# Three of eight row pairs of two matrix products by Strassen's algorithm, with all sums on VectorE

## The chip, the cores and the metric

One NeuronCore of a Trainium2 chip runs the whole program. The metric is the device time of one execution in microseconds (us). TensorE (PE) multiplies matrices into eight PSUM banks; VectorE (DVE) and ScalarE (ACT) do everything elementwise; GpSimd (POOL) does little here; SyncE (SP) issues the loads of the weights.

## The reference

The program is a trunk of two layers on x of 256 rows by 2048 columns (float32). Each layer has two halves:

```
u = RMSNorm(x)
proj = u @ w_in                                   # 2048 -> 8256
y_a = MLA(c_q, c_kv, k_pe) @ w_o_mla              # 8 heads
y_b = neighbourhood_attention(q, k, v) @ w_o_na   # 8 heads
merged = sigmoid(gate_a) * y_a + sigmoid(gate_b) * y_b
x = x + merged @ w_out                            # 2048 -> 2048
h = RMSNorm(x) @ w_ff1                            # 2048 -> 8192
x = x + square(relu(h)) @ w_ff2                   # 8192 -> 2048
```

A final RMSNorm gives the output.

## The kernel before

Matrix products are done in float32 from two rounded parts: a value is a high part (`hi`, a cast by ScalarE to the format that TensorE multiplies) and a low part (`lo`, value minus high part, by VectorE). A product takes high x high, high x low and low x high.

Weights come in blocks of 1 MB, by SyncE, into one of three `raw` tiles. `weights` (L157 and on) casts two rows of 128 k at a time: ScalarE writes `hi` (L172), VectorE `lo` (L173), each 128 x 1024, four tiles of either kind. Activations stand as `pair` tiles, high part and low part side by side, in 44 slots.

Two routines multiply. `gemm_a` (L215) holds the activations fixed in the array and streams 512 columns of weights: for each of 16 rows of k and each half t of the 256 rows three matmuls (L199, L200, L201) into one of two banks, 96 in all. It is used for the gates, the output projections, `w_out` and `w_ff2`, that is, for all products whose result has its rows on the partitions. `gemm_b` (L227) streams the activations against weights held fixed (L194, L195) into four banks; it makes the hidden values of the MLP, and the queries and keys.

The MLP goes in four blocks of 2048 hidden columns: four calls of `gemm_b` with w_ff1, whose results `relu2` squares and splits, and then four calls of `gemm_a` with w_ff2, whose results `residual` adds to x with the squared norm scale (L619, one instruction for each bank). For w_out the sum is L617.

Small steps that other work must not wait for (transposes of the merged branches and of x, attention heads, norm scales) are generators in a list; `tick`, called between matmuls, advances one of them when its lag has passed, and `drain` runs them all. In this way the transposes of each quarter of `merged` start while the next quarter is still being multiplied, and the scales of a layer's norm are made while the next layer's first product runs. Three banks (`abank`) are kept for these steps and five for the products.

The order of instructions on each engine is set afterwards by a scheduler, which takes dependences, free buffers and its own estimates; each engine runs its list in that order.

Of the kernel before, what the change touches and what calls it, by code (L numbers as in the profile page):

```python
# [54 lines left out]
NSLOT, ABANKS, SMALL, RBUFS, HBUFS = 44, 3, 8, 3, 4  # L56
# [6 lines left out]
def trunk(ctx: ExitStack, tc: tile.TileContext, x, w_in, w_uq, w_ukv, rpb, w_o_mla, w_o_na,  # L63
# [3 lines left out]
    wpool = ctx.enter_context(tc.tile_pool(name="wpool", bufs=4))  # L67
    slots = ctx.enter_context(tc.tile_pool(name="slots", bufs=NSLOT))
    tmp = ctx.enter_context(tc.tile_pool(name="tmp", bufs=2))
    psum = ctx.enter_context(tc.tile_pool(name="psum", bufs=8, space=bass.MemoryType.PSUM))  # L70

    def bank():
        return psum.tile([P, 512], F32, tag="bank", name="bank", bufs=8 - ABANKS)

    def abank():
        return psum.tile([P, 512], F32, tag="abank", name="abank", bufs=ABANKS)
# [8 lines left out]
    def small():  # L85
        return tmp.tile([P, S], F32, tag="small", name="small", bufs=SMALL)
# [70 lines left out]
    def weights(w, nk, c0, n, before=None):  # L157
# [3 lines left out]
        for k0 in range(0, nk, 2):  # L161
# [6 lines left out]
            hi = wpool.tile([P, 1024], F32R, tag="hi", name="hi", bufs=HBUFS)  # L168
            lo = wpool.tile([P, 1024], F32R, tag="lo", name="lo", bufs=HBUFS)
# [6 lines left out]
    def weights_twice(w, nk, c0, n):  # L176
# [4 lines left out]
        for k0 in range(0, nk, 8):  # L181
            hi = wpool.tile([P, 1024], F32R, tag="hi", name="hi", bufs=HBUFS)
            lo = wpool.tile([P, 1024], F32R, tag="lo", name="lo", bufs=HBUFS)
# [58 lines left out]
    def rows_of(col):  # L242

        dg = [tmp.tile([P, P], F32, tag="diag", name="diag", bufs=4) for _ in range(2)]
# [6 lines left out]
        row = tmp.tile([P, S], F32, tag="rrow", name="rrow", bufs=4)  # L251
        nc.vector.tensor_copy(row, pb[:, :S])
        return row

    def root(v, width, name):

        nc.vector.tensor_scalar(v, v, 1.0 / width, EPS, op0=ALU.mult, op1=ALU.add)  # L257
        col = tmp.tile([P, 2], F32, tag="rcol", name=name, bufs=6)
# [3 lines left out]
    class Norm:  # L262
# [5 lines left out]
        def add(self, t):  # L268
# [6 lines left out]
            nc.gpsimd.tensor_tensor(self.acc, self.acc, sq, op=ALU.add)  # L275

        def scales(self):
# [5 lines left out]
            v = tmp.tile([P, 2], F32, tag="var", name="var", bufs=2)  # L283
# [4 lines left out]
    class RowNorm:  # L288


        def __init__(self):
            self.sums = tmp.tile([P, 2, 4], F32, tag="sums", name="sums", bufs=2)

        def add(self, t, c4):
            junk = tmp.tile([P, 512], F32, tag="junk", name="junk", bufs=1)
# [3 lines left out]
        def scale(self):  # L299
            v = tmp.tile([P, 2], F32, tag="var", name="var", bufs=2)  # L300
# [3 lines left out]
        def scales(self):  # L304

            self.scale()
            self.half = tmp.tile([P, 2], F32, tag="rcol", name="half", bufs=6)
# [3 lines left out]
        def square(self):  # L311

            self.scale()
            self.sq = tmp.tile([P, 2], F32, tag="rcol", name="sq", bufs=6)
            nc.vector.tensor_tensor(self.sq, self.col, self.col, op=ALU.mult)
            return
            yield
# [157 lines left out]
    for l in range(DEPTH):  # L475
        wi = w_in[l]
# [116 lines left out]
        mg = [None] * NC  # L593
        for c4 in range(4):
            th = [None] * 2

            def merge(t, ps):
# [3 lines left out]
                if t == 1:  # L601
                    start(turned(lambda t, c4=c4: part[t, c4], c4, mg, lambda c: 0.5), 2)
# [4 lines left out]
            gemm_a(w_o_mla[l], c4 * 512, att, merge)  # L607


        last = l == DEPTH - 1  # L610

        def residual(c4, scale=None, n=None, then=None):

            def evac(t, ps):
                cs = xt[t][:, c4 * 512:(c4 + 1) * 512]
                if scale is None:
                    nc.vector.tensor_tensor(cs, cs, ps, op=ALU.add)  # L617
                else:
                    nc.vector.scalar_tensor_tensor(cs, ps, scale.sq[:, t:t + 1], cs, op0=ALU.mult, op1=ALU.add)  # L619
                if n is not None:  # L620
                    n.add(t, c4)
                if then is not None and t == 1:
                    start(then(c4), 2)
# [4 lines left out]
        for c4 in range(4):  # L628
            gemm_a(w_out[l], c4 * 512, mg,
                   residual(c4, None, mlp, lambda c4, xg=xg: turned_x(c4, xg, G_MLP + l * NC)))  # L630
        start(mlp.square(), 10)
# [4 lines left out]
        for b in range(NB):  # L636
            hid = []

            def relu2(m, ps):
                t = whole(ps)  # L640
                nc.vector.scalar_tensor_tensor(t, t, 0.0, t, op0=ALU.max, op1=ALU.mult)  # L641
                a = pair()
                split(a, t)
                hid.append(a)

            for c4 in range(4):
                gemm_b(w_ff1[l], b * D + c4 * 512, xg, relu2)
            for c4 in range(4):
                if b < NB - 1:
                    ev = residual(c4, mlp)  # L650
                elif last:
                    ev = residual(c4, mlp, norm)
                else:
                    ev = residual(c4, mlp, norm, lambda c4, nxt=nxt: turned_x(c4, nxt, G_MIX + (l + 1) * NC))
                gemm_a(w_ff2[l][b * D:(b + 1) * D, :], c4 * 512, hid, ev)
            if last and b == NB - 2:
                gfin = [wide() for _ in range(4)]
                for c4 in range(4):
                    nc.gpsimd.dma_start(gfin[c4], gain_fin[:, c4 * 512:(c4 + 1) * 512].to_broadcast([P, 512]))
        xg = nxt  # L660
        if not last:
            start(norm.scales(), 10)

# [67 lines left out]
```

## Time and profile before

| | |
|---|---|
| time, median of 3 runs (lowest to highest) | 2689.91 us (2688.54 to 2690.1) |
| the profiled execution's own time | 2689.91 us |
| its span in the profile | 2688.1 us |
| busy, PE / DVE / ACT / POOL | 2666.8 / 1602.9 / 1277.1 / 60.5 us |
| HBM traffic | 492 MB read, 184 GB/s over the span |

The own time holds 1.8 us around the span. "Busy" counts the union of an engine's instructions. Matmul rows overlap one another, so the cost of one is the step from start to start. In a group's row, the count is followed by busy time and mean length of one, then by the engine's idle time just before these instructions and by what ended it.

### The profile page before, as it was taken

The page shows a single profiled execution, that of the slowest core. Times are in us where ns is not written, and L with a number is a line of the kernel's source. Part 1 is how long each engine was busy: PE and PEld are TensorE (multiplying, and loading weights), DVE is VectorE, ACT ScalarE, POOL GpSimd, SP SyncE. Part 2 cuts the span into 40 slices and gives each one's busy share as a digit, 9 for nine tenths or more (in the row PEclk, how much of TensorE's full clock was granted, in tenths as well). Part 3 has the DMA queues.
Part 4 walks back from the last instruction along what each step waited for, and adds up shares of the span by engine and source line. Part 5 has one row for each costly group of instructions (what it writes and reads, how often), then busy time and mean ns, then how long its engine had stood idle before and what let it go on. Part 6 is the DMA issues. An engine that isn't in the chain of part 4 may idle for free.

```text
span 2688.1 us, 34037 instructions
## 1 busy us (share of the span) xinstructions
PE 2666.8 (99%) x13596; PEld 2268.7 (84%) x13596; DVE 1602.9 (60%) x2158; ACT 1277.1 (48%) x1815; POOL 60.5 (2%) x86
## 2 busy tenths in 40 slices
PE   8999999999999999999999999999999999999998
PEld 7888888888888888888888888888888888888886
DVE  5676486555655546556567754955556555565554
ACT  5554465444434434444445544644444344443443
POOL 1110000000000000000001100000000000000000
PEclk9999999999999999999999999999999999999999
DMA  7555644555565555555555555455555555655554
GB/s 231 184 165 189 195 161 155 189 184 180 186 203 186 190 190 186 197 193 189 183 183 179 171 187 183 153 167 188 188 188 188 189 187 194 208 189 193 188 188 141
DMA packets 253839, 496.49 MB, mean 185 GB/s; under 512 B 12688, under 2 KB 16784, under 8 KB 253680
## 3 DMA queue, kind: packets, MB, share of 16 engines
q1 hardware_dynamic: 250624, 488.14, 55.2%
q0 software_dynamic: 2048, 4.56, 0.6%
q8 instruction: 106, 1.74, 0.3%
q10 hardware_dynamic: 1008, 1.61, 0.2%
q14 instruction: 53, 0.43, 0.0%
HBM read 492.18 MB, written 2.10 MB: 184 GB/s over the span
## 4 chain that ended last, share of the span: by engine, by line
PE 84%; issue 14%; DVE 1%; DMA 1%; ACT 0%; POOL 0%; SPq 0%; POOLq 0%; DVEq 0%; ACTq 0%
PE bank L194 21%; PE bank L199 16%; PE bank L200 16%; PE bank L201 16%; PE bank L195 11%; DMA raw<-in_w_in 1%; PE abank L206 1%; PE abank L205 1%; PE abank L204 1%; PE abank L326 1%; PE abank L377 0%; DVE lo L173 0%; DVE wide L670 0%; PE abank L347 0%; ACT hi L172 0%
## 5 line engine op out<-in xcount | busy, mean ns | idle before, releaser
L173 DVE TENSOR_TENSOR lo<-raw,hi 128x1024 fp32r<-128x1024 f32 (+1 forms) x928 | 1132.5, 1222 | 977.8 <-ACT hi L172 973.0
L172 ACT CAST hi<-raw 128x1024 fp32r<-128x1024 f32 (+1 forms) x928 | 971.8, 1049 | 1131.1 <-PE bank L201 736.2
L194 PE MATMUL bank<-pair,hi 128*128 128x512 f32 x3008 | 1059.0, 398 | 2.3 <-DVE small L212 1.0
L200 PE MATMUL bank<-lo,pair 128*128 128x512 f32 (+1 forms) x2240 | 866.1, 387 | 0.0
L199 PE MATMUL bank<-hi,pair 128*128 128x512 f32 (+1 forms) x2240 | 865.8, 388 | 0.0
L201 PE MATMUL bank<-hi,pair 128*128 128x512 f32 (+1 forms) x2240 | 865.8, 387 | 0.0
L195 PE MATMUL bank<-pair,lo 128*128 128x256 f32 x3008 | 835.5, 280 | 0.4 <-DVE lo L173 0.3
L194 PEld LDWEIGHTS bank<-pair,hi 128*128 128x128 f32 x3008 | 563.5, 188 | 133.0 <-ACT hi L172 1.9
L195 PEld LDWEIGHTS bank<-pair,lo 128*128 128x128 f32 x3008 | 567.7, 189 | 5.9 <-DVE lo L173 1.6
L201 PEld LDWEIGHTS bank<-hi,pair 128*128 128x128 f32 x2240 | 420.8, 188 | 84.6
L199 PEld LDWEIGHTS bank<-hi,pair 128*128 128x128 f32 x2240 | 420.8, 188 | 84.1
L200 PEld LDWEIGHTS bank<-lo,pair 128*128 128x128 f32 x2240 | 420.9, 188 | 82.6
L150 ACT ACTIVATE pair<-small 128x256 fp32r<-128x256 f32 x200 | 73.6, 413 | 89.8 <-DVE small L641 67.1
L210 ACT COPY small<-bank 128x256 f32<-128x256 f32 x218 | 78.6, 369 | 29.0 <-PE bank L195 27.8
L152 DVE TENSOR_TENSOR pair<-small,pair 128x256 fp32r<-128x256 f32 x200 | 76.6, 418 | 19.2 <-ACT pair L150 19.2
L212 DVE TENSOR_TENSOR small<-bank,small 128x256 f32<-128x256 f32 x218 | 83.0, 416 | 0.2
L259 POOL TENSOR_TENSOR col<-var,mhalf 128x2 f32<-128x2 f32 x9 | 6.3, 702 | 1928.8 <-DVE var L257 1928.8
L619 DVE SCALAR_TENSOR_TENSOR xt<-bank,sq,xt 128x512 f32<-128x512 f32 x64 | 45.0, 744 | 7.8 <-PE bank L201 7.8
L641 DVE SCALAR_TENSOR_TENSOR small<-small 128x256 f32<-128x256 f32 x128 | 48.2, 418 | 0.0
L154 DVE SCALAR_TENSOR_TENSOR pair<-abank,g_sb,pair 128x256 fp32r<-128x256 f32 x64 | 29.2, 478 | 23.0 <-ACT pair L150 23.0
L150 ACT ACTIVATE pair<-abank,g_sb 128x256 fp32r<-128x256 f32 x64 | 28.2, 469 | 27.3 <-PE abank L326 23.4
L150 ACT ACTIVATE pair<-abank 128x256 fp32r<-128x256 f32 x64 | 23.6, 381 | 29.2 <-PE abank L206 19.1
(96 smaller groups left out, 789.9 us busy)
## 6 DMA issues: line engine op xcount, KB each, us to landing
raw<-in_w_ff SPq DMA_DIRECT2D x256, 1024.0 KB, 5.0
raw<-in_w_in SPq DMA_DIRECT2D x124, 1024.0 KB, 5.1
raw<-in_w_out SPq DMA_DIRECT2D x32, 1024.0 KB, 4.9
raw<-in_w_o_na SPq DMA_DIRECT2D x16, 1024.0 KB, 4.9
raw<-in_w_o_mla SPq DMA_DIRECT2D x16, 1024.0 KB, 4.9
raw<-in_w_ukv SPq DMA_DIRECT2D x8, 1024.0 KB, 4.9
raw<-in_w_uq SPq DMA_DIRECT2D x8, 768.0 KB, 4.6
raw<-in_w_in SPq DMA_DIRECT2D x10, 512.0 KB, 4.9
```

The lines of the kernel that those rows point to most:

```text
L150: nc.scalar.activation(dst[:, :S], src, AF.Copy, scale=scale)
L152: nc.vector.tensor_tensor(dst[:, S:], src, dst[:, :S].bitcast(F32), op=ALU.subtract)
L172: nc.scalar.copy(hi, src)
L173: nc.vector.tensor_tensor(lo, src, hi.bitcast(F32), op=ALU.subtract)
L194: nc.tensor.matmul(ps, wh, a, start=first, stop=False)
L195: nc.tensor.matmul(ps[:, :S], wl, a[:, :S], start=False, stop=last)
L199: nc.tensor.matmul(ps, a[:, t * P:(t + 1) * P], wh, start=first, stop=False)
L200: nc.tensor.matmul(ps, a[:, t * P:(t + 1) * P], wl, start=False, stop=False)
L201: nc.tensor.matmul(ps, a[:, S + t * P:S + (t + 1) * P], wh, start=False, stop=last)
L210: nc.scalar.copy(h, ps[:, S:])
L212: nc.vector.tensor_tensor(t, ps[:, :S], h, op=ALU.add)
L641: nc.vector.scalar_tensor_tensor(t, t, 0.0, t, op0=ALU.max, op1=ALU.mult)
```

## The change

**The products.** `gemm_s` takes the place of `gemm_a` for w_out and w_ff2, on 1024 columns at a time, so each of these products is two calls (g = 0, 1) where it was four. It goes through eight pairs of k rows. Pairs 0, 1, 3, 5 and 7 are plain: 24 matmuls into four banks (numbers 2, 3, 4, 8). Pairs 2, 4 and 6 (`SPAIRS`) take the 2 x 2 blocks of activations and weights through Strassen's algorithm in Winograd's form: seven products of three matmuls, into banks 1 to 7. For it VectorE makes four sums of weight blocks (t1 and t3 in one instruction, t2, t4) and, once per block of activations, four sums of activation blocks (s1 to s4, in `operand`). The results of the Strassen pairs and of the plain pairs share banks 2, 3 and 4. `evac` adds all into x by twelve VectorE instructions and one ScalarE copy.

**The weights.** In this half of the layer the `hi` and `lo` tiles are 128 x 2048, three of each; a Strassen pair uses two (1536 and 2048 elements), a plain pair one.

**Memory.** The pools `wpool` and `tmp` are opened anew for each half of a layer, the second half's at addresses of the first's. All eight banks are one pool.

**Order.** The transposes of `merged` are started only when the first half has been drained; at the end of the first layer all steps are drained before the second layer begins. The norm scale is applied in `relu2`, ahead of the square, and not at the sum into x; `Norm.add` sums on VectorE and no longer on GpSimd.

```diff
+SPAIRS = (2, 4, 6)
...
     def bank():
-        return psum.tile([P, 512], F32, tag="bank", name="bank", bufs=8 - ABANKS)
+        return psum.tile([P, 512], F32, tag="bank", name="bank", bufs=8)
+    abank = bank
...
+    def operand(f, strassen):
+        a11, a21, a12, a22, s1, s2, s3, s4 = (f[:, i] for i in range(8))
+        if strassen:
+            nc.vector.tensor_tensor(s1, a21, a22, op=ALU.add)
+            nc.vector.tensor_tensor(s2, s1, a11, op=ALU.subtract)
+            nc.vector.tensor_tensor(s4, a12, s2, op=ALU.subtract)
+            nc.vector.tensor_tensor(s3, a21, a11, op=ALU.subtract)
...
+    def turned_pair(src, c, dst, j):
...
+        f = tmp.tile([P, 8, P], F32, tag="f", name="f", bufs=2)
+        nc.scalar.activation(f[:, :4].rearrange("p a q -> p (a q)"), tp, AF.Copy, scale=0.5)
+        dst[j] = operand(f, j in SPAIRS)
...
+    def gemm_s(w, c0, acts, evac):
...
+        for j in range(n):
+            raw = wpool.tile([P, 2048], F32, tag="raw", name="raw", bufs=RBUFS)
...
+            if j not in SPAIRS:
+                ws = parts(raw)
...
+                    for i, t, side in ((2, 0, right), (3, 0, left), (4, 1, right), (8, 1, left)):
+                        mm3(i, ah[2 * k + t], al[2 * k + t], *side)
...
+                continue
...
+            nc.vector.tensor_tensor(ts[:, :2], b12.rearrange("p (a n) -> p a n", a=1).to_broadcast([P, 2, 512]),
+                                    raw[:, 512:1536].rearrange("p (a n) -> p a n", a=2), op=ALU.subtract)
+            nc.vector.tensor_tensor(t2, b22, t1, op=ALU.subtract)
+            nc.vector.tensor_tensor(t4, b21, t2, op=ALU.subtract)
+            w11, w22, w21 = parts(raw[:, 512:])
+            w1, w3, w2, w4 = parts(ts.rearrange("p a n -> p (a n)"))
...
+            mm3(1, a11, l11, *w11)
+            mm3(2, a12, l12, *w21)
+            mm3(3, s4, r4, *w22)
+            mm3(5, s1, r1, *w1)
+            mm3(7, s3, r3, *w3)
+            mm3(6, s2, r2, *w2)
+            mm3(4, a22, l22, *w4)
+        evac(b)
...
-                if t == 1:
-                    start(turned(lambda t, c4=c4: part[t, c4], c4, mg, lambda c: 0.5), 2)
...
+        drain()
+        half_a.close()
...
+        hbufs, smalls = 3, 3
+        wpool = half_b.enter_context(tc.tile_pool(name="wpool2", bufs=4, reuse_waits="tile"))
+        tmp = half_b.enter_context(tc.tile_pool(name="tmp2", bufs=2, reuse_waits="tile"))
+        for c4 in range(4):
+            for c in range(2):
+                start(turned_pair(lambda t, c4=c4: part[t, c4], c, mg, 2 * c4 + c), 0)
...
-                    nc.vector.scalar_tensor_tensor(cs, ps, scale.sq[:, t:t + 1], cs, op0=ALU.mult, op1=ALU.add)
+                nc.scalar.copy(p1, b[1])
+                nc.vector.tensor_tensor(u2, p1, b[6], op=ALU.add)
+                put(x11, p1)
+                nc.vector.tensor_tensor(u4, u2, b[5], op=ALU.add)
+                put(x12, u4)
+                nc.vector.tensor_tensor(u3, u2, b[7], op=ALU.add)
+                put(x21, u3)
+                nc.vector.tensor_tensor(x22, x22, b[5], op=ALU.add)
+                put(x22, u3)
+                nc.vector.tensor_tensor(x12, x12, b[3], op=ALU.add)
+                nc.vector.tensor_tensor(x11, x11, b[2], op=ALU.add)
+                nc.vector.tensor_tensor(x22, x22, b[8], op=ALU.add)
+                nc.vector.tensor_tensor(x21, x21, b[4], op=ALU.add)
...
         if not last:
             start(norm.scales(), 10)
+            while pending:
+                drain()
+        half_b.close()
```

The scheduled order shows the change at three places. First VectorE, in a block's product with w_ff2, where one stretch of columns gives way to the next. `lo` are low parts, `t` the sums of weight blocks, `xt` is x, `wide` holds the u. Before, L619 is the whole sum into x:

```order
L173 TENSOR_TENSOR lo<-raw,hi 128x1024 x7
L619 SCALAR_TENSOR_TENSOR xt_91<-bank,sq,xt_91 128x512
L619 SCALAR_TENSOR_TENSOR xt_92<-bank,sq,xt_92 128x512
L173 TENSOR_TENSOR lo<-raw,hi 128x1024 x8
L619 SCALAR_TENSOR_TENSOR xt_91<-bank,sq,xt_91 128x512
L619 SCALAR_TENSOR_TENSOR xt_92<-bank,sq,xt_92 128x512
```

And now, from the last pairs of g = 0 to the first of g = 1:

```order
L383 TENSOR_TENSOR lo<-raw,hi 128x2048
L732 TENSOR_TENSOR xt_88<-xt_88,wide 128x512
L739 TENSOR_TENSOR wide<-wide,bank 128x512
L383 TENSOR_TENSOR lo<-raw,hi 128x2048
L741 TENSOR_TENSOR wide<-wide,bank 128x512
L743 TENSOR_TENSOR wide<-wide,bank 128x512
L745 TENSOR_TENSOR xt_89<-xt_89,bank 128x512
L383 TENSOR_TENSOR lo<-raw,hi 128x2048
L748 TENSOR_TENSOR xt_88<-xt_88,bank 128x512
L732 TENSOR_TENSOR xt_88<-xt_88,wide 128x512
L405 TENSOR_TENSOR t<-raw 128x1024
L732 TENSOR_TENSOR xt_89<-xt_89,wide 128x512 x2
```

The low parts of the next pairs stand between the sums into x of the last ones, and the t sums among them.

Second, ScalarE where the first half of layer 0 passes into the second. `th` is the gate's tanh, L150 casts transposed pieces of `merged`. Before:

```order
L172 CAST hi<-raw 128x1024 x4
L533 ACTIVATE th<-bank,half 128x512 x2
L172 CAST hi<-raw 128x1024 x7
L150 ACTIVATE pair<-abank 128x256 x3
L172 CAST hi<-raw 128x1024
L150 ACTIVATE pair<-abank 128x256
L172 CAST hi<-raw 128x1024 x5
```

And now, where L355 copies transposed pieces into f and L341 casts them:

```order
L643 ACTIVATE th<-bank,half 128x512 x2
L189 CAST hi<-raw 128x1024
L355 ACTIVATE f<-bank 128x512
L341 CAST pair<-f 128x512
L382 CAST hi<-raw 128x2048 x2
L355 ACTIVATE f<-bank 128x512
L341 CAST pair<-f 128x512
```

The casts of w_out's first weights now stand behind the first piece of `merged`, whose tile f lies where `th` lay.

Third, TensorE at the end of layer 0. Before, the norm's scales (L250) fall between matmuls of the next layer's first product:

```order
L195 MATMUL bank<-pair,lo 128x256
L194 MATMUL bank<-pair,hi 128x512
L195 MATMUL bank<-pair,lo 128x256
L250 MATMUL abank<-diag,ones 128x128 x2
L194 MATMUL bank<-pair,hi 128x512
L195 MATMUL bank<-pair,lo 128x256
```

And now (L377 is the last product, L432 transposes x, L267 makes the scales, L211 is the next layer's first matmul):

```order
L377 MATMUL bank<-lo,pair 128x512
L377 MATMUL bank<-hi,pair 128x512
L432 MATMUL bank<-ident,xt_88 128x128 x4
L432 MATMUL bank<-ident,xt_89 128x128
L432 MATMUL bank<-ident,xt_88 128x128
L432 MATMUL bank<-ident,xt_89 128x128 x2
L432 MATMUL bank<-ident,xt_88 128x128
L432 MATMUL bank<-ident,xt_89 128x128 x2
L432 MATMUL bank<-ident,xt_88 128x128
L432 MATMUL bank<-ident,xt_89 128x128 x2
L432 MATMUL bank<-ident,xt_88 128x128
L432 MATMUL bank<-ident,xt_89 128x128
```

These transposes, and the first of the two matmuls of the scales behind them, stand ahead of the next layer's first matmul.

More of the change, by code (lines that the diff above doesn't have):

```diff
@@ L607, in trunk @@
             gemm_a(w_o_mla[l], c4 * 512, att, merge)
+        drain()
+        half_a.close()
         last = l == DEPTH - 1
[L612 to L623, printed above, removed]
+        half_b = ExitStack()
@@ L627, in trunk, with scaled_mlp @@
         xg = [None] * NC
[L628 to L631, printed above, removed]
+        for g in range(2):
+            gemm_s(w_out[l], g * 1024, mg,
+                   residual(g, mlp, lambda c4, xg=xg: turned_x(c4, xg, G_MLP + l * NC)))
+        def scaled_mlp():
+            start(mlp.scales(), 0)
+            while not hasattr(mlp, "row"):
+                advance(len(pending) - 1)
         norm = RowNorm()
```

166 lines of the change are left out of this document (122 added, 44 removed).

## The prediction

> **What bounds the kernel now.** I read the page's shares and slices first, then TensorE's busy time between its first and last matmul, then the groups of instructions, then the timeline of single instructions.
>
> ```profile
> span 2688.1 us, 34037 instructions
> PE 2666.8 (99%) x13596; PEld 2268.7 (84%) x13596; DVE 1602.9 (60%) x2158; ACT 1277.1 (48%) x1815; POOL 60.5 (2%) x86
> PE   8999999999999999999999999999999999999998
> PEclk9999999999999999999999999999999999999999
> PE 84%; issue 14%; DVE 1%; DMA 1%; ACT 0%; POOL 0%; SPq 0%; POOLq 0%; DVEq 0%; ACTq 0%
> ...
> core 0: us, PE busy (x) PEld busy (x) DVE busy (x) ACT busy (x) POOL busy (x), PEclk, DMA share, GB/s
> 12.00:2676.00 2664.00, 2661.68 (x13577) 2265.40 (x13578) 1595.15 (x2145) 1270.51 (x1802) 53.49 (x68) 1.00 0.56 185
> 731.00:820.00 89.00, 89.00 (x400) 73.89 (x399) 46.98 (x47) 34.20 (x34) 0.00 (x0) 1.00 0.57 191
> ```
>
> From 12 to 2676 us TensorE is idle for 2.3 us in all. In one block's second MLP product (731 to 820) it never stops, at a granted clock of 1.00, while VectorE works 47 of 89 us. So TensorE's matmul stream is the time, and the ends of the span hold the rest. A matmul saved is saved whole, and any new wait of TensorE is paid whole: nothing hides it.
>
> What one matmul costs is read from start to start, since the durations overlap:
>
> ```profile
> 2667.69 0.39 PE L201 MATMUL bank<-hi,pair 128*128 128x512 f32 x1
> ...
> 2675.85 0.39 PE L201 MATMUL bank<-hi,pair 128*128 128x512 f32 x1
> ```
>
> Between these lie 36 steps: 8.16 / 36 = 0.2267 us each, not the 0.39 us of a row.
>
> **The saving.** A plain pair of k rows over 1024 columns is 24 matmuls (5.44 us), a Strassen pair 7 x 3 = 21 (4.76 us). A product has three of them: 183 matmuls (41.5 us) for 192. There are 20 products (two of w_out and eight of w_ff2 in each layer): 180 fewer matmuls, 180 x 0.2267 = -40.8 us. Transposes keep their number.
>
> **VectorE within a product.** These rows price it; the trace has no 1536- or 2048-wide instruction, so I extend the two widths shown.
>
> ```profile
> L173 DVE TENSOR_TENSOR lo<-raw,hi 128x1024 fp32r<-128x1024 f32 x912 | 1117.4, 1226 | 972.5 <-ACT hi L172 967.7 <-PE bank L195 1.0
> L173 DVE TENSOR_TENSOR lo<-raw,hi 128x768 fp32r<-128x768 f32 x16 | 15.1, 954 | 5.3 <-ACT hi L172 5.3
> L172 ACT CAST hi<-raw 128x1024 fp32r<-128x1024 f32 x912 | 958.6, 1052 | 1123.9 <-PE bank L201 730.3 <-PE bank L194 363.2 <-issue 12.4
> L172 ACT CAST hi<-raw 128x768 fp32r<-128x768 f32 x16 | 13.2, 835 | 7.2 <-PE bank L201 5.9 <-PE bank L194 1.2
> L617 DVE TENSOR_TENSOR xt<-xt,bank 128x512 f32<-128x512 f32 x16 | 10.2, 681 | 0.0
> 821.51 2.36 DVE L173 TENSOR_TENSOR lo<-raw,hi 128x1024 fp32r<-128x1024 f32 x2 [3.24 <-ACT hi L172]
> raw<-in_w_ff SPq DMA_DIRECT2D x256, 1024.0 KB, 5.0
> ```
>
> On VectorE 256 elements more cost 0.272 us: 1536 take 1.77, 2048 take 2.31. On ScalarE they cost 0.217 us: 1.49 and 1.92. A plain pair is one low part, 2.31. A Strassen pair is t1 with t3 (1.23), t2 and t4 (0.68 each) and low parts of 1.77 and 2.31: 6.67. Twelve sums into x and u are 12 x 0.68 = 8.2. A product: 5 x 2.31 + 3 x 6.67 + 8.2 = 39.8 us, against TensorE's 41.5. Two low parts in a row take 2.36, not 2.45: the second costs 1.13. With 0.09 less on each of 32 instructions it is 36.9. VectorE goes from a half to about nine tenths of a product, and TensorE stays the longer. ScalarE has 5 x 1.92 + 3 x 3.41 = 19.8.
>
> So the sums are hidden by TensorE's products, if each pair's operands come in time. Three places decide:
> - The ring of three hi and three lo tiles: a Strassen pair holds two, a plain pair one. The plain pair after next can be cast when the plain pair before it ends, so cast and low part, 1.92 + 2.31 = 4.23, must fit into the 4.76 us of the Strassen pair between. Margin 0.5: cost 0. If VectorE is busy when the cast ends, the margin is gone.
> - The seventh pair's raw tile is free only after the fourth's low part, and a load lands 5.0 us after its issue. From that low part's end to the end of the next plain low part pass the load (5.0), three t sums (2.6) that stand ahead of it in VectorE's order, and itself (2.3): 9.9 us of a cycle of 5.44 + 4.76 = 10.2. It fits, barely: cost 0.
> - From a block's first 1024 columns to its second. After the last Strassen pair of the first VectorE owes, by its order, the 12 sums (7.2 at 0.6), two plain low parts (4.4), one low part of 1.7 and five t sums of the next pairs (3.5) before the new first Strassen pair's second cast may start: 16.8 us, begun some 0.5 us before that last pair ends. Then the cast, 1.9, and its low part, 2.2: 20.4 us after the pair's end. TensorE gets there after three plain pairs (16.3), nine matmuls (2.0) and the eight that need only high parts (1.8): 20.1. It waits about 0.3 us. With the sums in place before the pair ends (four of its eight banks are done one plain pair before the others) it waits nothing; if VectorE starts 1.2 us later, 1.5 us.
>
> I take 0.5 us for each product, since the other two margins are of that size too and will not hold everywhere: 20 x 0.5 = +10. The ends are 0 and 20 x 1.5 = 30. A gain is excluded: TensorE can't be under its matmuls.
>
> The doubled loads (4 KB rows, same bytes), the operand sums in the first MLP product (four of 128 elements a Strassen pair) and Norm's sums on VectorE lie under TensorE, where VectorE has 40% free: 0. The shared eight banks: 0; without that cover, a bank wait of one evacuation, 0.7 us.
>
> **The border from the first half of a layer to the second.** The transposes of the merged branches no longer lie between products. The tile f lies where th was, so its first copy waits for the last merge sum.
>
> ```profile
> L599 DVE SCALAR_TENSOR_TENSOR th<-th,bank 128x512 f32<-128x512 f32 x16 | 10.2, 681 | 1.3 <-PE bank L201 1.3
> L600 DVE TENSOR_TENSOR wide<-wide,th 128x512 f32<-128x512 f32 x16 | 10.3, 685 | 0.0
> L379 ACT CAST pp<-abank 128x512 fp32r<-128x512 f32 x32 | 18.7, 584 | 17.3 <-PE abank L377 17.1
> ```
>
> The merge of half t=0 starts 6 matmuls (1.36) before the last one ends and takes 0.68 + 0.68: it ends with it. Then ScalarE, in its order, copies f (0.58), casts it (0.58) and only then casts the first weights (1.92): 3.1 us in which TensorE has nothing. Behind it the first Strassen pair's second low part and the next plain pair's come about 0.5 us late each, three times: 1.5. Per layer 4.6, two layers +9.2; bounds 2 x 2.5 (casts alone) and 2 x 8.
>
> **The end of a layer** (once) **and of the kernel.** All four last sums, the squares, the scales and 16 transposes now stand on TensorE's queue ahead of the next layer's first matmul; before, other matmuls covered them.
>
> ```profile
> 2676.45 0.63 ACT L296 ACTIVATE junk<-xt 128x512 f32<-128x512 f32 x1 [9.31 <-DVE xt L619]
> 2676.98 0.19 ACT L296 ACTIVATION_READ_ACCUMULATOR junk<-xt 128x1 f32 x1
> 2678.56 0.16 DVE L301 TENSOR_REDUCE var<-sums 128x2 f32<-128x8 f32 x1 [0.85 <-ACT junk L296]
> 2679.76 5.39 DVE L670 SCALAR_TENSOR_TENSOR wide<-xt,col,wide 128x512 f32<-128x512 f32 x8 [0.83 <-POOL col L259]
> ```
>
> From the last matmul: four sums 2.5, three squares of 0.72 (0.53 + 0.19) and a split's 0.4 in ScalarE's order, 2.6; reduce to scale 2679.76 - 2678.56 = 1.2; the two diagonals 0.6: 6.9, less 16 transposes of 0.11 that are work anyway: 5.2, +5.5 with the first low part. Bounds 3 and 8. At the very end the reduce came 2.3 us after the last matmul (2675.85 + 0.39) and now comes after 2.5 + 2.4: +2.6, bounds 1 and 4.
>
> **Sum.** The profiled execution's own time, 2689.91, is also the runs' median. 2689.9 - 40.8 + 10 + 9.2 + 5.5 + 2.6 = 2676.4; I say 2676. Lower ends: 2689.9 - 40.8 + 0 + 5 + 3 + 1 = 2658. Upper ends: -40.8 + 30 + 16 + 8 + 4 = +17, 2707.
>
> **Rivals.**
> 1. *VectorE becomes the bound: slower.* If a Strassen pair's 6.67 us do not run ahead but must fit into the plain pair before it (5.44), each costs 1.23, 60 of them 74: 2676 - 10 + 74 = 2740. It decides from (40.8 - 17.3) / 60 = 0.39 us a pair. For it: 39.8 of 41.5, a margin of 0.5 in the ring, and casts and low parts that hand over to each other in order. Against it: the 972.5 us that low parts waited were for casts, not for VectorE, and back to back they cost less.
> 2. *Everything arrives in time.* 0 within the products, borders of 3.1: 2689.9 - 40.8 + 6.2 + 5.5 + 2.6 = 2663.
> 3. *TensorE's stalls slow its clock.* The trace shows it once, at the start:
>
> ```profile
> 4.48 0.66 PE L326 MATMUL abank<-ident,xt 128*128 128x128 f32 x2 [4.48 <-DMA xt<-in_x]
> 14.40 0.63 PE L194 MATMUL bank<-pair,hi 128*128 128x512 f32 x1
> 14.83 0.63 PE L195 MATMUL bank<-pair,lo 128*128 128x256 f32 x2
> 17.39 0.41 PE L195 MATMUL bank<-pair,lo 128*128 128x256 f32 x1
> 19.90 0.40 PE L194 MATMUL bank<-pair,hi 128*128 128x512 f32 x1
> ```
>
> After idle stretches a 512-wide matmul takes 14.83 - 14.40 = 0.43 us, and the rows stay long until 17.4, 5 us after the stream began at 12.3 (the clock column says 1.00 all the same). Such a phase costs 5 x (1 - 0.2267 / 0.43) = 2.4 us; if the two borders and the layer's end (3 to 5 us each) bring it on, 3 x 2.4 = 7: 2683. The Trainium skill, "TensorE: Matmul & The Clock Gate", Part 1, says so: after one idle window of about 3.4 us the array runs at half rate until some 3.4 us of steady work. By that rule a border's 3.1 us is just short and the layer's end is over it, one phase, 2679. The trace agrees on the half rate; it has no gap of 3 to 5 us inside the stream.
>
> **How the numbers follow.** A measurement here tells 0.2% (5.4 us) from no change. My forecast (2664 to 2692) has 0.50, rival 2 has 0.20, rival 3 0.14, rival 1 0.16. Under 2684.5 lie rival 2, most of the forecast (0.44), and 0.09 of rival 3, with a hundredth of rival 1: 0.74. Within 0.2%: 0.13, from the forecast's late end, rival 3 and a light rival 1. Slower: 0.13. The range from 2658, all lower ends together, to 2696 leaves out 0.13 of rival 1 and a few hundredths elsewhere.
>
> **What would show it.** Right: 3660 matmuls at the line of the products, a step of 0.227 inside a plain pair, VectorE busy 85 to 95% of a product, TensorE idle some 3 us at each half's border and 5 at the layer's end, and half a microsecond at the third pair of the second halves. Wrong: long waits of TensorE for low parts in the middle of products (rival 1), steps of 0.43 after the borders (rival 3), or a wait for banks at the start of a product. A VectorE instruction slower at 2048 elements than two of 1024, or when its sources include a bank, would upset the sum most.

## The result and the profile after

The changed kernel takes 2734.72 us (2732.66 to 2735.57, four runs) against 2689.94: a ratio of 1.0167, interval 1.0149 to 1.0184. It is slower by 45 us, where 14 us faster was forecast. The profiled execution took 2732.66 us, 42.75 more than that of before.

The page after:

```profile
span 2730.9 us, 33381 instructions
PE 2662.7 (98%) x13424; PEld 2242.0 (82%) x13424; DVE 1935.9 (71%) x2358; ACT 1377.7 (50%) x1701; POOL 52.0 (2%) x74
...
PE   8999999999999999999999999999999999999997
...
PE 82%; issue 8%; DVE 5%; DMA 3%; ACT 2%; POOL 0%; POOLq 0%; DVEq 0%; ACTq 0%
...
L377 PE MATMUL bank<-hi,pair 128*128 128x512 f32 x2440 | 769.1, 394 | 16.9 <-ACT hi L382 15.8
...
L377 PE MATMUL bank<-lo,pair 128*128 128x512 f32 x1220 | 480.4, 394 | 10.4 <-DVE lo L383 10.2
```

The 180 matmuls are gone (2440 + 1220 = 3660 of the products), yet TensorE is busy for 4 us less only, in a span that is 43 us longer. So there are two losses to find: idle time, and busy time that fewer matmuls fill. The view of waits has the first (before, only the wait for x at the start, 7.4 us, was over 1.0 us in all):

```profile
engine line waited for: us in total, times, longest us
PE bank L377 <- ACT hi L382: 15.8, 17, 3.1
PE bank L377 <- DVE lo L383: 10.2, 13, 1.4
PE bank L211 <- DVE pair L162: 7.9, 4, 2.9
PE bank L432 <- DMA xt<-in_x: 6.3, 2, 4.3
PE bank L267 <- DVE diag L263: 4.9, 1, 4.9
```

For the second, windows over single products help, since nothing waits in the first 1024 columns of a block's product with w_ff2 (columns: window, its length, then busy time and count of PE, PEld, DVE, ACT, POOL, granted clock, DMA share, GB/s):

```profile
748.69:790.58 41.89, 41.89 (x185) 34.41 (x184) 33.55 (x34) 23.18 (x20) 0.00 (x0) 1.00 0.52 178
924.92:1010.41 85.49, 84.88 (x370) 68.72 (x369) 71.25 (x66) 43.03 (x32) 0.00 (x0) 1.00 0.55 189
```

The first window is such a half, the second a whole product of a block. 183 matmuls in 41.89 us are 0.2289 us each, at a granted clock of 1.00: before it was 0.2267. The same 1% lies on matmuls whose code did not change. In the stage of the gates before (first fence) and after (second), the step from start to start is 1.59 / 7 = 0.227 and 1.83 / 8 = 0.229:

```profile
500.01 0.39 PE L199 MATMUL bank<-hi,pair 128*128 128x512 f32 x1
...
501.60 0.39 PE L200 MATMUL bank<-lo,pair 128*128 128x512 f32 x1
```

```profile
499.80 0.39 PE L216 MATMUL bank<-hi,pair 128*128 128x512 f32 x1
...
501.63 0.39 PE L218 MATMUL bank<-hi,pair 128*128 128x512 f32 x1
```

Over the whole trace three such matmuls without a wait take 0.6870 us in the mean (before 0.6806). In `gemm_b` a matmul of 512 columns and one of 256 follow each other; such a couple takes 0.3530 us (before 0.3504). The program has 6348 of the former matmuls and 3008 couples: 6348 / 3 x 0.0064 + 3008 x 0.0026 = 21 us.

VectorE is busy 71.25 us in a block's product of 85.49, 35.6 for each half in the mean: a little under the forecast's lower figure of 36.9. The halves differ, though: 33.6 in the first and 37.7 in the second, which also makes the first one's sums into x.

### The profile page after: what moved, and what is told of

Read it like the earlier page. It is cut to its first block, busy times and chain, and to the rows that moved or that the text cites. A ratio compares the mean times of both kernels' runs of the same rounds, so it can differ in the third digit from the quotient of the medians.

```text
span 2730.9 us, 33381 instructions
## 1 busy us (share of the span) xinstructions
PE 2662.7 (98%) x13424; PEld 2242.0 (82%) x13424; DVE 1935.9 (71%) x2358; ACT 1377.7 (50%) x1701; POOL 52.0 (2%) x74
## 3 DMA queue, kind: packets, MB, share of 16 engines
q0 software_dynamic: 2048, 4.56, 0.6%
## 4 chain that ended last, share of the span: by engine, by line
PE 82%; issue 8%; DVE 5%; DMA 3%; ACT 2%; POOL 0%; POOLq 0%; DVEq 0%; ACTq 0%
PE bank L211 23%; PE bank L377 20%; PE bank L212 12%; PE bank L216 8%; PE bank L218 8%; PE bank L217 8%; DVE lo L383 2%; ACT hi L382 1%; DMA raw<-in_w_ff 1%; DMA raw<-in_w_out 1%; PE bank L221 1%; PE bank L223 1%; PE bank L222 1%; DMA raw<-in_w_in 1%; DVE t L405 1%
## 5 line engine op out<-in xcount | busy, mean ns | idle before, releaser
L211 PE MATMUL bank<-pair,hi 128*128 128x512 f32 x3008 | 1071.8, 400 | 12.5 <-DVE pair L162 7.9
L377 PE MATMUL bank<-hi,pair 128*128 128x512 f32 x2440 | 769.1, 394 | 16.9 <-ACT hi L382 15.8
L211 PEld LDWEIGHTS bank<-pair,hi 128*128 128x128 f32 x3008 | 566.8, 189 | 147.0 <-DVE pair L162 8.9
L190 DVE TENSOR_TENSOR lo<-raw,hi 128x1024 fp32r<-128x1024 f32 (+1 forms) x352 | 426.5, 1214 | 352.6 <-ACT hi L189 351.9
L189 ACT CAST hi<-raw 128x1024 fp32r<-128x1024 f32 (+1 forms) x352 | 364.3, 1041 | 415.4 <-PE bank L218 309.0
L377 PEld LDWEIGHTS bank<-hi,pair 128*128 128x128 f32 x2440 | 457.4, 188 | 123.3 <-ACT hi L382 25.4
L377 PE MATMUL bank<-lo,pair 128*128 128x512 f32 x1220 | 480.4, 394 | 10.4 <-DVE lo L383 10.2
L182 DVE TENSOR_TENSOR lo<-raw,hi 128x2048 fp32r<-128x2048 f32 x128 | 293.2, 2291 | 202.5 <-ACT hi L181 202.5
L383 DVE TENSOR_TENSOR lo<-raw,hi 128x2048 fp32r<-128x2048 f32 (+1 forms) x160 | 331.1, 2088 | 107.9 <-ACT hi L382 107.9
L382 ACT CAST hi<-raw 128x2048 fp32r<-128x2048 f32 (+1 forms) x160 | 277.5, 1750 | 249.8 <-PE bank L377 200.1
L181 ACT CAST hi<-raw 128x2048 fp32r<-128x2048 f32 x128 | 244.3, 1910 | 265.3 <-PE bank L211 230.9
L216 PE MATMUL bank<-hi,pair 128*128 128x512 f32 (+1 forms) x960 | 370.8, 387 | 0.0
L218 PE MATMUL bank<-hi,pair 128*128 128x512 f32 (+1 forms) x960 | 369.8, 386 | 0.0
L217 PE MATMUL bank<-lo,pair 128*128 128x512 f32 (+1 forms) x960 | 367.0, 382 | 0.0
L377 PEld LDWEIGHTS bank<-lo,pair 128*128 128x128 f32 x1220 | 229.4, 188 | 67.4 <-DVE lo L383 18.5
```

The lines of the kernel that those rows point to most:

```text
L181: nc.scalar.copy(his, raw)
L182: nc.vector.tensor_tensor(los, raw, his.bitcast(F32), op=ALU.subtract)
L189: nc.scalar.copy(hi, src)
L190: nc.vector.tensor_tensor(lo, src, hi.bitcast(F32), op=ALU.subtract)
L211: nc.tensor.matmul(ps, wh, a, start=first, stop=False)
L216: nc.tensor.matmul(ps, a[:, t * P:(t + 1) * P], wh, start=first, stop=False)
```

## Experiments: the longer step

Casts, low parts and sums have their former lengths, so the slow step is TensorE's alone. What differs for the unchanged code is where its tiles lie. Before, weight and activation tiles all started on multiples of 256 bytes of their partition. After, the activations do, and the weight tiles start 64 bytes past one.

**Pools in the other order** (the kernel before):

```diff
-    wpool = ctx.enter_context(tc.tile_pool(name="wpool", bufs=4))
     slots = ctx.enter_context(tc.tile_pool(name="slots", bufs=NSLOT))
+    wpool = ctx.enter_context(tc.tile_pool(name="wpool", bufs=4))
```

> The kernel before with the pool of activation tiles placed below the pool of weight tiles (as after), all starts still on multiples of 256 bytes; no instruction moves. In the trace of after every TensorE step is 0.9% longer than before (three matmuls of 512 columns 0.687 us for 0.6805, in stages whose code did not change too). Theory 1, a tile's start not on a multiple of 256 bytes does it (after: weight tiles at 64 past one): here nothing changes, 2690 us, 0.6805. Theory 2, which of weights and activations lies lower does it: 0.687 and 2690 + 22 = 2712 us. Theory 3, neither (the wider tiles or the shared banks): 2690 us.

2689.0 us, ratio 1.000 (0.9991 to 1.0009); three matmuls 0.681. Which of the two lies lower is of no account here.

**The changed kernel aligned**, by a tile of 192 bytes ahead of the weights:

```diff
     tmp = wpool = None
+    shift = keep.tile([P, 48], F32, tag="shift", name="shift", bufs=1)
+    nc.vector.memset(shift, 0.0)
```

> The changed kernel with 192 bytes of padding, so that weight tiles start on multiples of 256 bytes; no instruction moves (one small memset is added). Theory 1 (alignment): steps back to 0.6805 for three, 2735 - 22 = 2713 us. Theories 2 and 3: 0.687 and 2735 us.

2721.2 us, ratio 1.012 (1.0104 to 1.0135), 13.5 less than the changed kernel (2713 had been expected). The first half of the same product now takes 41.51 / 183 = 0.2268 a matmul:

```profile
741.93:783.44 41.51, 41.51 (x186) 34.35 (x185) 33.53 (x34) 23.26 (x21) 0.00 (x0) 1.00 0.52 180
```

Not all of the 21 us came back: TensorE reaches its waits earlier (those of the products grow by 5 us, table below), and the couples' mean came down only to 0.3517 (4 us). Block by block they differ: in each layer's first MLP product the couples now take 0.3475 in the mean, in the products of the other blocks 0.353 as in the changed kernel. One such product of 256 couples, in the changed and in the aligned kernel (before: 89.67):

```profile
834.72:924.92 90.20, 90.20 (x513) 78.32 (x512) 61.10 (x71) 44.19 (x51) 0.00 (x0) 1.00 0.60 196
827.19:917.38 90.19, 90.19 (x513) 78.23 (x512) 61.22 (x71) 44.20 (x51) 0.00 (x0) 1.00 0.59 196
```

So the starts explain the longer step of the products by Strassen and of the gates, and of the couples only a part.

**Activations on the other side of the memory, and everything shifted by 32 bytes:**

```diff
-    slots = ctx.enter_context(tc.tile_pool(name="slots", bufs=NSLOT))
-    keep = ctx.enter_context(tc.tile_pool(name="keep", bufs=2))
+    slots = ctx.enter_context(tc.tile_pool(name="slots", bufs=NSLOT, side="right"))
+    keep = ctx.enter_context(tc.tile_pool(name="keep", bufs=2, side="right"))
```

> The changed kernel with the activation tiles at the upper end of the memory and the weight tiles below them, as in the kernel before; weight tiles now start on multiples of 256 bytes, activation tiles 32 bytes short of one; no instruction moves. Theory 1 (alignment): still 0.687 or so, since one side is off, 2735 us (between 2713 and 2735 if only the weights' start counts). Theory 2 (which lies lower): 0.6805 and 2713 us. Theory 3: 2735 us.

```diff
+    shift = const.tile([P, 8], F32, name="shift")   # kernel before, ahead of all weight and activation tiles
```

> The kernel before with every weight and activation tile 32 bytes past a multiple of 256 (64 did not fit into the memory); no instruction moves. Theory 1 (alignment): 0.687 for three matmuls and 2690 + 22 = 2712 us. Theories 2 and 3: 0.6805 and 2690 us.

The first takes 2751.1 us (ratio 1.0227, 1.0211 to 1.0242), slower than any theory had it, with 0.700 for three matmuls; the second 2688.2 us (ratio 0.9996, 0.9986 to 1.0005), with 0.681. So a start off a multiple of 256 bytes does no harm if all tiles are off alike: theory 1 as I had put it is wrong, and what is left is the start of one operand against the other.

**Activations alone shifted** by 32 bytes, in the kernel before (a pool of 32 bytes between `wpool` and `slots`):

> The kernel before with the activation tiles alone 32 bytes further on (weight tiles on multiples of 256 bytes, activation tiles 32 past one); no instruction moves. Theory 1, narrowed: what counts is how the two operands of a matmul start against one another (0 in before and when all were shifted by 32 bytes together; 64 in after; 32 with the sides changed, where three matmuls took 0.700 us). Then three matmuls take 0.700 here and a 512+256 couple 0.352: 2689 + 6528 x 0.0065 + 3008 x 0.0019 = 2737 us. Rival, the slow steps belong to the changed kernel (shared banks, wider tiles) and the shift only trimmed them: 2689 us.

2720.4 us, ratio 1.0116 (1.0101 to 1.0131). Three matmuls take 0.700 as expected, with no instruction moved: of the changed kernel nothing is needed for the slow step. The couples went the other way from what I expected (0.352), to 0.347. The products of a block, the second and the next block's first (before: 87.07 and 89.67):

```profile
736.02:825.62 89.60, 89.60 (x387) 72.14 (x385) 47.10 (x50) 35.30 (x37) 0.00 (x0) 1.00 0.56 187
825.62:914.46 88.84, 88.84 (x513) 78.63 (x512) 52.56 (x72) 42.51 (x59) 0.00 (x0) 1.00 0.58 190
```

6528 x 0.0065 - 3008 x 0.0033 = +32 us; 31 were measured.

**Only the faster half of that**: the weight tiles of `gemm_b`, and those of the queries and keys, 32 bytes short, in the kernel before. The longer tiles got their room from a smaller `dynamic_dma_scratch_size`, here and in the next run; the products with w_ff2 keep their 87.05 us with it.

```diff
-    hi, lo = (t[:, :2 * n] ...)
+    hi, lo = (t[:, off:off + 2 * n] ...)      # abridged; off = 56 (224 bytes) in gemm_b, 0 in gemm_a; tiles 256 bytes longer
```

> The kernel before with the weight tiles of the products with weights held fixed (queries, keys, hidden values) starting 32 bytes short of a multiple of 256, all else on multiples of 256; no instruction moves. With the activations alone 32 bytes further on, the 512+256 couples had taken 0.347 instead of 0.350 us and the other products 0.233 a matmul instead of 0.227. If the start of one operand against the other is what counts, the couples take 0.347 here and the other products 0.227: 2689 - 3008 x 0.0033 = 2679 us. Rival, it is the activations' own start: 2689 us.

2679.9 us, ratio 0.9965 (0.9952 to 0.9978): the kernel before gains 9.4 us with the same instructions in the same order. Its blocks show 87.05 and 88.84:

```profile
726.21:813.26 87.05, 87.05 (x386) 72.10 (x385) 46.99 (x50) 35.36 (x37) 0.00 (x0) 1.00 0.56 192
813.26:902.10 88.84, 88.84 (x514) 78.64 (x513) 52.63 (x72) 42.52 (x59) 0.00 (x0) 1.00 0.58 191
```

**A start for each block:**

> The kernel before with another start of the weight tiles in each of the eight MLP blocks (four a layer): 16, 32, 64, 96, 128, 160, 192 and 224 bytes past a multiple of 256, for both products of the block; activations stay on multiples of 256, as do the weights of all other products; no instruction moves. Known so far, from whole kernels: 0 takes 87.07 us for a block's second product and 89.67 for its first; weights 64 past took 0.687 for three matmuls of the second kind (87.9 us a block), activations 32 past 0.700 (89.6), weights 32 short 0.347 for a couple of the first kind (88.9). Theory, a period of 64 bytes: 64, 128 and 192 are like 0, the others like 32. Theory, a period of 256: 64 gives 87.9, 192 too, 128 something of its own. If starts were of no account within one kernel, all eight blocks take 87.07 and 89.67.

2705.1 us, ratio 1.006 (1.0037 to 1.0083). Windows of the blocks' second products with weights 16, 32, 64, 128, 160 and 192 bytes past (the 96 block also carries the layer's last transposes; 224 takes 89.59):

```profile
727.18:816.14 88.96, 88.96 (x386) 72.21 (x385) 47.07 (x50) 35.19 (x37) 0.00 (x0) 1.00 0.57 189
906.52:996.12 89.60, 89.60 (x386) 71.98 (x385) 47.06 (x50) 35.17 (x37) 0.00 (x0) 1.00 0.57 188
1086.51:1174.41 87.90, 87.90 (x386) 72.12 (x385) 46.98 (x50) 35.14 (x37) 0.00 (x0) 1.00 0.56 190
2066.03:2155.26 89.23, 89.23 (x386) 72.35 (x385) 47.04 (x50) 35.18 (x37) 0.00 (x0) 1.00 0.55 188
2244.91:2334.88 89.97, 89.97 (x387) 72.32 (x385) 47.06 (x50) 35.21 (x37) 2.23 (x4) 1.00 0.60 198
2424.66:2514.27 89.61, 89.61 (x386) 72.20 (x385) 47.04 (x50) 35.27 (x37) 0.00 (x0) 1.00 0.55 187
```

Both theories fall as they were put: 128 is not like 0, so the period is not 64 bytes, and 192 is not like 64, as the second had it. Of the starts tried, 0 is the best for these products (87.07), 64 next (87.90), the others cost 2 to 3%. For the couples the means are 0.347 at 16, 96 and 224 and 0.350 to 0.353 at the other five. Weights 224 bytes past stand to the activations as with activations 32 bytes past, and both runs agree (0.700 and 0.347). Why the step depends on it is open, and so is what else the couples depend on.

## Experiments: the waits

As in the forecast, a product is 1024 columns, a half of w_out or of a block's w_ff2. The table adds up, for each kind of product, what the steps of its matmuls are over 0.2267 us (us in all; steps of transposes in between are left out; stretches at half the clock, told of below, are in it). "Aligned" is the changed kernel with the 192 bytes; the two right columns are runs that follow.

| products | after | aligned | no t sums | two pairs in second half |
|---|---|---|---|---|
| w_out, first halves (2) | 8.4 | 9.1 | 3.0 | 8.1 |
| w_out, second halves (2) | 11.3 | 11.1 | 2.6 | 1.6 |
| w_ff2, first halves (8) | 3.3 | 0.0 | 0.0 | 0.1 |
| w_ff2, second halves (7) | 14.8 | 14.4 | 0.0 | 0.0 |
| the same, last block of layer 0 | 6.2 | 6.2 | 2.0 | 2.3 |
| sum | 44 | 41 | 8 | 12 |

Of the 44 after, 8 are the longer step (20 x 183 x 0.0023); 36 are waits. The cause in a second half, VectorE's timeline (ScalarE's cast and TensorE's wait behind it, each from its own timeline; the last fence has the same cast in the aligned kernel):

```profile
970.91 1.29 DVE L732 TENSOR_TENSOR xt<-xt,wide 128x512 f32<-128x512 f32 x2
972.11 1.75 DVE L383 TENSOR_TENSOR lo<-raw,hi 128x1536 fp32r<-128x1536 f32 x1
973.78 0.68 DVE L747 TENSOR_TENSOR xt<-xt,bank 128x512 f32<-128x512 f32 x1
974.38 0.69 DVE L407 TENSOR_TENSOR t<-raw,t 128x512 f32<-128x512 f32 x1
974.98 0.68 DVE L750 TENSOR_TENSOR xt<-xt,bank 128x512 f32<-128x512 f32 x1
975.58 0.68 DVE L749 TENSOR_TENSOR xt<-xt,bank 128x512 f32<-128x512 f32 x1
976.18 1.22 DVE L405 TENSOR_TENSOR t<-raw 128x1024 f32<-128x1024 f32 x1
977.31 0.69 DVE L408 TENSOR_TENSOR t<-raw,t 128x512 f32<-128x512 f32 x1
```

```profile
978.11 1.91 ACT L382 CAST hi<-t 128x2048 fp32r<-128x2048 f32 x1 [9.31 <-PE bank L377]
```

```profile
981.87 0.97 PE L377 MATMUL bank<-hi,pair 128*128 128x512 f32 x3 [0.61 <-ACT hi L382]
```

```profile
970.17 1.91 ACT L382 CAST hi<-t 128x2048 fp32r<-128x2048 f32 x1 [9.40 <-DVE t L408]
```

VectorE works without a gap: the sums into x of the half that ended, and the next half's t sums among and behind them. The last t sum of the first Strassen pair (L408) ends at 978.0, and the cast of the sums starts at 978.11. TensorE waits for it, and then for the plain pair's cast that stands behind it on ScalarE: the 0.61 us. The cast's row names TensorE, where a matmul ended 0.04 us after that t sum; in the aligned kernel the same cast's row names the t sum. The next run settles it.

**Without the t sums** (aligned; the four blocks are cast as loaded, which leaves out part of the product):

```diff
-            w1, w3, w2, w4 = parts(ts.rearrange("p a n -> p (a n)"))
+            w1, w3, w2, w4 = parts(raw)
```

> The aligned changed kernel (2721 us) with the t sums of the weight blocks left out: the four blocks are cast as they were loaded. Leaves out part of the product. VectorE is 2.6 us lighter for each Strassen pair, and the second cast of a pair waits for the load alone. In the aligned kernel the 20 products lose 40.9 us in waits: 25 in the products with w_out and the last block of the first layer, 14 in the second halves of the others. Theory A, VectorE's sums come late everywhere: the waits fall below 12 us, 2721 - 29 = 2692 us. Theory B, in w_out and the last block it is the transposes and their casts and the banks: only the 14 go, 2707 us.

2689.2 us: 32 less, and 33 of the 41 us of waits are gone, those of w_out and of the last block too. Theory A: the late weight sums eat 32 of the 40.8 us that the matmuls save. The kernel without them only draws level with the one before (ratio 1.0001, 0.9992 to 1.001), so the rest of the saving goes at the borders, in the first MLP products, at the ends and in stretches at half the clock, all told of below.

**The t sums on GpSimd** (aligned; `nc.gpsimd` for `nc.vector` in the three t instructions):

> The aligned changed kernel with the t sums of the weight blocks on GpSimd instead of VectorE. GpSimd's one wide instruction in the trace takes 1.01 us for 384 elements, so 2560 elements a Strassen pair take 6.7 us of a cycle of 10.2. Theory A: the sums are done early, since a pair's block lands 10 us before its casts, and VectorE is relieved: near the run without them, 2695 us. Rival: GpSimd is late or slows VectorE beside it, waits for casts of the sums in every Strassen pair: 2721 + 60 x 0.3 = 2740 us or more.

2763.8 us, ratio 1.0277 (1.0259 to 1.0294): the rival, and worse than its 2740. GpSimd is late (26 of the 60 casts of sums wait for its last one), and VectorE is slower beside it. A pair's sums take 2.85 + 2.27 + 2.17 = 7.3 us, and VectorE's low parts of 1536 elements, 1752 ns in the aligned kernel, take 2447 ns beside them:

```profile
L405 POOL TENSOR_TENSOR t<-raw 128x1024 f32<-128x1024 f32 x60 | 170.7, 2846 | 1752.2 <-DMA raw<-in_w_ff 996.0 <-DMA raw<-in_w_out 386.8 <-DVE th L709 312.4
...
L383 DVE TENSOR_TENSOR lo<-raw,hi 128x1536 fp32r<-128x1536 f32 x60 | 146.8, 2447 | 12.9 <-ACT hi L382 12.9
```

**Two Strassen pairs in the second halves** (aligned):

```diff
-                gemm_s(w_ff2[l][b * D:(b + 1) * D, :], g * 1024, hid, ev)
+                gemm_s(w_ff2[l][b * D:(b + 1) * D, :], g * 1024, hid, ev, SPAIRS[g:])   # so for w_out
```

> The aligned changed kernel (2721 us) with only pairs 4 and 6 by Strassen in the second 1024 columns of each product, so that its first t sums come two plain pairs later; the first 1024 columns stay at 2, 4 and 6. 10 products x 3 matmuls more, +6.8 us. In the aligned kernel the ten second halves lose 31.6 of the 40.9 us. Theory A, the waits come from the 12 sums of the first half standing ahead of the t sums of the second's first Strassen pair: the second halves' waits fall below 1 us each (w_out and the last block included), 2721 + 7 - 25 = 2703 us. Rival, they belong to the second pair's load and to the transposes, which stay: 2721 + 7 - 10 = 2718 us.

2709.6 us, between the two; the mechanism is theory A's, the time is not. The second halves' waits fall from 31.7 to 4 us, 2.3 of them in the last block of layer 0. Less the 6.8 us of matmuls that should have been 21 us, and 11.6 came. At the layer's end the wait for the scales is 8.8 us instead of 4.9, with a longer phase at half the clock behind it, and the first MLP products grew by 2.9 and 2.6 us: the waits came back at the next places. Behind its waits 27 us of this run went by at a granted clock of 0.50, 14 us in the aligned kernel.

```profile
PE bank L267 <- DVE diag L263: 8.8, 1, 8.8
```

**w_out by the old routine** (aligned; `gemm_a` and the transposes of `merged` within the first half, as before):

> The aligned changed kernel with w_out by the old routine, in the first half of the layer, and with the transposes of merged started within it, as in the kernel before; the products with w_ff2 stay as they are. 36 matmuls more (+8.2 us). Theory A: the four products' waits (20.2), the waits at the halves' border (2 x 3.3 and two phases at half the clock, 2 x 1.7) and 3 to 4 us at each first MLP product go: 2721 + 8 - 20 - 10 - 6 = 2693 us. Rival: the border and its waits move to the first MLP product, whose first weights now wait for the first half's tiles: 2721 + 8 - 20 = 2709 us.

2706.0 us, ratio 1.0063 (1.0048 to 1.0078): near the rival's 2709. The w_out products' waits and the border's are gone, but the first MLP product now waits 3.4 us in each layer for its first cast weights:

```profile
PE bank L211 <- ACT hi L181: 6.8, 2, 3.4
```

**All together**: w_out as before, two pairs in second halves, no wait for all steps at the layer's end, the start of `gemm_b`'s weights as in the fast run of before.

> All that the runs point to: the run with w_out by the old routine (2706 us), with pairs 4 and 6 alone in the second halves of the products with w_ff2, without the wait for all steps at the first layer's end, and with the weight tiles of the hidden values, queries and keys 32 bytes short of a multiple of 256. Expected: 2706 - 15 (second halves) - 7 (layer's end, with one phase at half the clock) - 10 to 16 (couples) = 2670 us, 20 below the kernel before. Rival: the products' waits return elsewhere and the layer's end only moves: 2690 us.

2676.1 us, ratio 0.995 (0.9933 to 0.9966), nearer to the 2670 expected than to the rival: 13 us below the kernel before, of which the weights' start, which that kernel can have as well, gives 9.4 alone. Against that run (2679.9) the combination gains 4 us. The products with w_ff2 no longer wait (0.4 us in all). The layer's end kept its wait under another name, the next layer's first weights (4.9 of the 10.1 us in the first row; the other 5.2 are at the start of the program):

```profile
PE bank L211 <- ACT hi L189: 10.1, 2, 5.2
PE bank L211 <- ACT hi L181: 6.8, 2, 3.4
...
PE bank L377 <- ACT hi L382: 0.4, 1, 0.4
```

## Why the prediction was wrong

**The saving.** 180 matmuls went, each saved whole: right. But the sum took the step of before for all matmuls of the changed kernel. This price of a matmul is the first part of the forecast that failed: +21 us that stood in no term and no rival. The aligned kernel shows 13.5 of it in the time, and 5 more that came back as waits. The pools were moved, and I asked of that only what waits for whose tile.

**The products' late operands**, +10 with 30 as the upper end: 36 measured. This is the second part that failed. Of the three places the last was right: for w_ff2 the chain at the second half gave 0.3 to 1.5 us, and 1.1 to 1.5 came at its first Strassen pair; with up to 0.7 at the plain pair behind the second Strassen pair, and 0.4 of longer steps, such a half lost 1.8 to 2.6. First halves wait nothing, so the other two margins held there. The term failed because all 20 products were priced like these. In w_out and in the last block of layer 0 VectorE also makes the low parts of the transposed pieces, between the same sums:

```profile
602.96:651.70 48.74, 45.02 (x200) 35.80 (x199) 41.12 (x41) 25.97 (x28) 0.00 (x0) 1.00 0.51 176
553.66:602.96 49.30, 47.63 (x211) 38.56 (x212) 44.39 (x49) 30.95 (x30) 0.00 (x0) 0.97 0.49 174
```

The rows are the second and the first half of layer 0's w_out: 41 and 44 us of VectorE, not 36.9 to 39.8 (the second half of the last block: 41.5). These five products carry 24 of the 36 us. Either of the two was enough to leave the range, which ended at 2696, below the sum's own upper end of 2707: the longer step alone would have put the forecast at 2676.4 + 21 = 2697, and the aligned kernel, without it, still takes 2721.

**The border**, 3.1 us for two instructions of ScalarE and a cast: 3.14 measured. The later lateness of 1.5 was about 2, at the second Strassen pair and not the first; it is counted among the products above. **The layer's end**, 5.2: 0.47 + 4.87 measured. The order of instructions with durations from rows was enough for these. **The kernel's end**, +2.6: the reduce starts 3.9 us after the last matmul (2721.29 - 2717.43), not 2.3: +1.5.

```profile
2721.29 0.16 DVE L318 TENSOR_REDUCE var<-sums 128x2 f32<-128x8 f32 x1 [2.35 <-ACT junk L313]
```

The border's and the layer's end's waits in TensorE's timeline:

```profile
553.66 0.97 PE L377 MATMUL bank<-hi,pair 128*128 128x512 f32 x3 [3.14 <-ACT hi L382]
...
1367.43 2.04 PE L432 MATMUL bank<-ident,xt 128*128 128x128 f32 x16 [0.47 <-DVE xt L747]
1374.34 0.80 PE L267 MATMUL bank<-diag,ones 128*128 128x128 f32 x2 [4.87 <-DVE diag L263]
```

**A place left out**: the first MLP product, in each layer. It needs the transposes of all of x; w_out's last sums now cover half of x and stand among low parts on VectorE. TensorE waits 2.9 us twice.

```profile
667.75 0.80 PE L211 MATMUL bank<-pair,hi 128*128 128x512 f32 x1 [2.87 <-DVE pair L162]
```

**Rival 3** was right beside the forecast, not instead of it. Four phases of 3.41 us ran at a granted clock of 0.50, each at the end of a wait; three of them:

```profile
554.56:557.97 3.41, 3.41 (x17) 3.23 (x16) 3.41 (x2) 3.30 (x5) 0.00 (x0) 0.50 0.16 24
667.20:670.61 3.41, 2.86 (x9) 2.48 (x10) 2.25 (x6) 1.72 (x5) 0.00 (x0) 0.50 0.56 164
1373.77:1377.18 3.41, 2.84 (x9) 2.46 (x10) 3.41 (x6) 2.48 (x4) 0.43 (x1) 0.50 0.00 0
```

That is 4 x 1.7 = 7 us at most, some of it within the products' figure. The second layer's wait of 2.86 us before its first MLP product brought none, the first's of 2.87 did. The phases start a whole number of 3.413 us apart (667.20 - 554.56 = 33 of them, 1373.77 - 554.56 = 240), so where a wait falls on that grid decides. Cut into stretches of 3.413 us on that grid, the trace has four in which TensorE was idle for 2.0 us or more (2.51, 2.32, 3.41 and 2.85), each right ahead of one of these phases; no other was idle for more than 1.75. Of the wait of 2.87 us, 2.32 fell into one stretch; that of 2.86 was split into 1.12 and 1.73. The Trainium skill, "TensorE: Matmul & The Clock Gate", Part 1, has a free-running window of 3413 ns; these starts agree. That a wait must last a whole window, as the forecast read the skill, they do not bear out.

**Rival 1** named 2740 us, and 2735 came, but not in its way: VectorE does run ahead within a product, and no first half of w_ff2 waits for it. It is late where sums, t sums and transposes meet.

Together: -40.8 + 21 (step) + 36 (products) + 6 (borders) + 6 (first MLP products) + 5 (layer's end) + 1.5 (kernel's end) + up to 7 (clock) = 42, against 42.75. So close a sum is partly luck: the clock's 7 us lie partly within the products' 36, and smaller shifts of either sign, among them in the attention heads' stage, were not followed up.

## What to carry to other kernels

A change that opens pools anew or reorders them can move every tile: look at where the two operands of the hot matmul start against each other, before and after, and pad so that the difference stays, or try others. When work moves to an engine that is half idle on the average, price it in the stage where that engine also has its other work, by what stands ahead in its queue when the first consumer needs it; one Strassen pair fewer right after such a place was worth more than the matmuls that it cost. A wait that is removed at one border tends to come back at the next, so sum up the waits of the whole span before believing in the gain.

## What the hardware showed that I had not expected

With the same instructions, a matmul of 512 columns took 0.2267 us when its two operands started alike modulo 256 bytes, 0.229 with the weights 64 bytes past the activations and 0.233 with them 32 or 224 past. In the kernel before, couples of 512 and 256 columns took 0.350 when they started alike and 0.347 with the weights 16, 96 or 224 bytes past. All of it at a granted clock of 1.00. On the whole program that was +31 us (activations shifted) or -9 us (weights of the couples shifted).

A wait need not last a whole 3.413 us to bring on a phase at half the clock: in the changed kernel 2.3 us of idle time within one such stretch were followed by one, 1.75 were not.
